# The recurrence's weights loaded from GpSimd's own queue, and a head's output stores tied behind the next head's value products

## The chip, the cores and the metric

The kernel runs on one core of one Trainium2 chip. The metric is the time of one execution on the device in microseconds (us), the median of several runs. In the profile PE is TensorE (matmuls), PEld its weight load, DVE is VectorE, ACT ScalarE, POOL GpSimd and SP SyncE, whose instruction queue (SPq in the profile) issues most of the kernel's transfers.

## The reference

The model is a trunk of two layers on a sequence of 1024 tokens of width 1024 in float32. Layer 0 mixes tokens with forgetting attention (FoX, 16 heads), layer 1 with gated linear attention (GLA, 4 heads, keys of width 128, values of width 256); after each stands a SwiGLU channel mixer. Ahead of every sub-layer the rows are normalised (RMS) and modulated by scale, shift and gate computed from a conditioning vector c by the weights `ada_w`. The change is in layer 1's mixer:

```python
def gated_linear_attention(h, w_in, w_a2, b_a, g_o, w_out):
    proj = h @ w_in
    q, k, v, r, a_lr = jnp.split(proj, ...)          # 512, 512, 1024, 1024, 16 columns
    log_alpha = jax.nn.log_sigmoid(a_lr @ w_a2 + b_a) / GLA_TAU
    b = jnp.cumsum(log_alpha, axis=2)                # within a chunk of 64 tokens, by head
    b_last = b[:, :, -1]
    q_in, k_in = q * jnp.exp(b), k * jnp.exp(-b)
    A = jnp.where(tril, jnp.einsum('bnthk,bnshk->bnhts', q_in, k_in), 0.0)
    o_intra = jnp.einsum('bnhts,bnshv->bnthv', A, v)
    kv = jnp.einsum('bnshk,bnshv->bnhkv', k * jnp.exp(b_last[:, :, None] - b), v)
    # S_n = exp(b_last) * S_{n-1} + kv_n, carried from chunk to chunk
    o = o_intra + jnp.einsum('bnthk,nbhkv->bnthv', q_in, s_prev)
    o = o * lax.rsqrt(jnp.mean(o * o, axis=-1, keepdims=True) + EPS) * g_o
    return (o * jax.nn.silu(r)) @ w_out
```

## The kernel before

All products are made of pairs: a float32 value is split into a high part, rounded to the matmul's type, and a low part, what is left of it. `split` gives the high part to ACT (L163) and the low part to DVE (L164), and `mm3` (L241 to L243) makes a product of three matmuls: high by high, low by high, high by low. On-chip memory is a set of 54 slots of 4 KB a partition; a `Ring` hands the slots of a list out in turn, and a slot's next user waits for its last reader.

Each engine runs its instructions in one order. That order is not written by hand: the program is written once in source order, a scheduler that simulates time then orders each engine's instructions (`schedule_with_timeline_sim=True`), and `tc.issue_after(ins)` ties what stands in its block behind an instruction. DMAs stand in the queue of the engine that issues them, between its other instructions. The core is set up with `dynamic_dma_scratch_size=1024`, bytes reserved for the descriptors of transfers that GpSimd issues.

**Weights.** `load_w` (L194 to L210) loads one weight, 512 KB in either shape: 8 blocks of 128 rows by 128 columns, or 4 blocks of 128 rows by 256 columns. One DMA on SP's queue (L198) puts it into a raw buffer of a ring `wr` of three; ACT copies the high parts (L206), and four subtractions of 128x256 make the low parts (L209), all four or three of them on POOL, in the second case the fourth on DVE. `Weights.next` keeps three weights loaded ahead. The names tell which weight it is: `w__s` are those of keys, queries and gates r, `wv` those of values, `wo` the output weights (`_h` high, `_l` low). The ring, so named, has its readers on ACT, POOL and DVE.

**The stage.** Layer 1 begins at about 1300 us with the norm of the rows: half of the columns at a time, `rms_cols` sums squares on PE (`sp`, L531), DVE and POOL make the inverse root of it (`rs`, L534 and L535), and PE spreads this over partitions (`rb`, L543). Then the modulated rows `h1` are made, `h1h` by ACT (L563) and `h1l`, for the odd blocks, by POOL (L564). The second half of the tokens gets its norm while the products of the first half run. `gv_body` makes the values of a quarter of the tokens (`gv` on PE, split into `gvt`), `a_body` and `gate_z` the decay gates, and `r_proj` the output gate `gr` (Silu into the ring `gs` of two slots).

**The heads.** For each of the four heads `head_front` makes keys (`gk`) and queries (`gqp`). DVE multiplies a projection by the decay into one of two buffers `gy` (L1703 for the queries); from there ACT rounds the high parts (`kih`, `gq00h` and so on) and POOL subtracts the low part of the keys, `kil` (L1688); DVE makes the low part of the queries. So a buffer `gy` is free for the next projection when POOL has made `kil`. `head_back` makes scores (`at`), values under scores (`go`), the state (`kv`, by the transposed keys `kdh`, `kdl`) and the normalised outputs `gs`: the inverse root `gss` is POOL's (L1804), DVE scales, PE transposes (`ogt`, L1764), DVE multiplies it into `gs` (L1767). `head_end` finishes the last of these outputs and, for heads 0 to 2, stores two 128x1024 tiles of them on SP's queue (L1718). They are loaded again when the output product is made; those of head 3 stay on chip.

**Beside it.** Between the heads' instructions runs `ada1`, the modulation of what follows: SP loads a 128x512 tile of `ada_w` in four pieces (L361), ACT multiplies it by the condition (L379), POOL adds it to a sum (L381). Its tiles are a short ring, so SP waits for POOL there. The rows of `x` that the mixer's result is added to are put aside on SP's queue (`x_d`, L1550).

Of the kernel before, what the change touches and what calls it, by code (L numbers as in the profile page):

```python
# [16 lines left out]
P = 128  # L17
# [36 lines left out]
def trunk(ctx, tc, x, c, ada_w, ada_b, norm1_g, norm2_g, ffn_w_in, ffn_w_out,  # L54
          fox_w_in, fox_b_f, fox_w_out, gla_w_in, gla_w_a2, gla_b_a, gla_g_o,
          gla_w_out, final_g, out, dbg=None, stop=None):
    nc = tc.nc
    dbg = dbg or {}
# [53 lines left out]
    def run(g):  # L112
        for _ in g:
            pass
# [4 lines left out]
    def weave(a, ta, b, tb, lags=None):  # L119


        ca = cb = 0.0
        a_on = b_on = True
        bb = nc.cur_bb.bb.instructions
        hist = {e: [] for e in lags or ()}
        while a_on or b_on:
            n = len(bb)
            if a_on and (not b_on or ca * tb <= cb * ta):
                r = next(a, None)
                a_on = r is not None  # L130
                ca += r or 0.0
                for e, h in hist.items():
                    new = [i for i in bb[n:] if i.engine == ENG[e]]
                    h.append(new[-1] if new else h[-1] if h else None)
            else:
                r = next(b, None)
                b_on = r is not None
                cb += r or 0.0
                for e, h in hist.items():
                    if len(h) > lags[e] and h[-1 - lags[e]] is not None:  # L140
                        for i in bb[n:]:
                            if i.engine == ENG[e]:
                                tc.add_manual_dep(i, h[-1 - lags[e]].name, mybir.DependencyInfo(
                                    mybir.DependencyClass.NoSync, mybir.DependencyReason.DATA), reason="order")
# [17 lines left out]
    def split(hi, lo, src):  # L162
        nc.scalar.copy(hi, src)  # L163
        nc.vector.tensor_sub(lo, src, hi.bitcast(F32))  # L164
# [24 lines left out]
    def leave_ffn():  # L189
        if opr_:  # L190
            ws.q = deque(opr_["sg"] + list(opr_["r"].q))
            opr_.clear()

    def load_w(src, name, ws=ws, lo_p=3):  # L194

        kk, m = src.shape[0] // P, src.shape[1]
        raw = wr([P, kk, m], F32, name)
        nc.sync.dma_start(raw, src.rearrange("(k p) m -> p k m", p=P))  # L198
        leave_ffn()
        w = Pair(ws([P, kk, m], FR, name + "h"), ws([P, kk, m], FR, name + "l"))  # L200
        flat = lambda t: t.rearrange("p k m -> p (k m)")
        hi, lo, rw = flat(w.hi), flat(w.lo), flat(raw)
        n = kk * m
        for i in range(2):
            cs = slice(i * n // 2, (i + 1) * n // 2)
            nc.scalar.copy(hi[:, cs], rw[:, cs])  # L206
        for i in range(4):
            cs = slice(i * n // 4, (i + 1) * n // 4)
            (nc.gpsimd if i < lo_p else nc.vector).tensor_sub(lo[:, cs], rw[:, cs], hi[:, cs].bitcast(F32))  # L209
        return w  # L210
# [15 lines left out]
    class Weights:  # L226
# [7 lines left out]
        def next(self):  # L234
            while self.loads and len(self.got) < self.depth:
                f, *a = self.loads.popleft()
                self.got.append(f(*a))
            return self.got.popleft()
# [13 lines left out]
    def proj_tok(ps, w2, hs, t):  # L252

        ts_ = psl(t)
        for k in range(8):
            w = w2[k // 4]
            mm3(ps, hs[k].hi[:, ts_], hs[k].lo[:, ts_], w.hi[:, k % 4, :], w.lo[:, k % 4, :], k == 0, k == 7)
            yield 0.33
# [53 lines left out]
    W = fox_w_in[0]  # L312
    wf = load_w16(W[:, 3 * D:3 * D + 16], "fw", wst)
    wq0 = load_w(W[:, 0:P], "wq0", wst)
    wk0 = load_w(W[:, D:D + P], "wk0", wst)
    load_ada0(1)
    load_ada0(2)
# [27 lines left out]
    def last_of(e, n=0):  # L345
        return [i for i in nc.cur_bb.bb.instructions[-400:] if i.engine == ENG[e]][-1 - n]
# [83 lines left out]
    def ada1_queue(js, acc, raws_, ahead=1):  # L430
        r = Cycle(raws_)
        for j in js:
            ada1.q.append(ada_pair(1, j, lambda *_: acc, r, 1, ahead))
# [210 lines left out]
    def w_loads(wmat, lo, w=P):  # L644
        return [(load_w, wmat[:, lo:lo + w], f"w{lo}_")]
# [920 lines left out]
    ada_v = Views(take(2), 2, [HALF], "ad").v  # L1566
    ada1_queue((2, 4), ada_v[0], ada_v[1:4], 2)
    ADA_A, ADA_B, ADA_LAG = 2.5, 1.0, 6
    rm = cst.tile([P, HALF], BF16, name="rm")
    nc.vector.memset(rm, 1.0)  # L1570
    nc.vector.memset(rm.rearrange("p (n c) -> p n c", c=P)[:, :, 0:1], 0.0)
# [29 lines left out]
    def gv_body(h, wv, tp):  # L1601
        ps = pj([P, 2, 256], F32, f"gv{h}{tp}")
        for i in range(2):
            run(proj_tok(ps[:, i, :], wv, h1, 2 * tp + i))
        ada1(5.1)
        v = vr([P, 2, 2, 256], FR, f"gvt{h}{tp}")
        split(v[:, 0], v[:, 1], ps)
        return v
# [65 lines left out]
    def head_front(h, b16, t2, ei, nmid):  # L1674

        ahead = gate_ahead(h + 1) if h < 3 else iter(())
        wk = feed.next()
        kin = Pair(kir([P, S], FR, f"kih{h}"), kir([P, S], FR, f"kil{h}"))
        for hf in range(2):
            cs = hsl(hf)  # L1680
            ps = pj([P, HALF], F32, f"gk{h}{hf}")
            run(proj(ps, wk, h1, hf))
            ada1(5.1)
            y = yv()
            nc.vector.tensor_mul(y, ps, ei[:, cs])
            nc.vector.tensor_mul(t2[:, cs], ps, t2[:, cs])
            nc.scalar.copy(kin.hi[:, cs], y)
            nc.gpsimd.tensor_sub(kin.lo[:, cs], y, kin.hi[:, cs].bitcast(F32))  # L1688
            for n in range(4 * hf, 4 * hf + 4):
                nc.scalar.activation(ei[:, psl(n)], b16[:, psl(n)], AF.Exp, scale=1.0 / 16, bias=nmid[:, n:n + 1])  # L1690
            nc.scalar.activation(b16[:, cs], b16[:, cs], AF.Exp, scale=1.0 / 16)
            if h:
                next(ahead, None)
        wq = feed.next()
        qt = [Pair(qr([P, S], FR, f"gq{h}{i}h"), qr([P, S], FR, f"gq{h}{i}l")) for i in range(2)]
        for hf in range(2):
            cs = hsl(hf)
            ps = pj([P, HALF], F32, f"gqp{h}{hf}")
            run(proj(ps, wq, h1, hf))
            ada1(5.1)  # L1700
            for t, f in zip(qt, (ei, b16)):
                y = yv()
                nc.vector.scalar_tensor_tensor(y, ps, QS, f[:, cs], op0=ALU.mult, op1=ALU.mult)  # L1703
                split(t.hi[:, cs], t.lo[:, cs], y)
            if not h:
                next(ahead, None)
        return kin, qt
# [4 lines left out]
    def head_end(h, gs):  # L1712

        run(last_og.popleft())
        for dv in range(2):
            gtile[2 * h + dv] = gs[dv]
            if h < 3 or "og" in dbg:
                nc.sync.dma_start(og_d[2 * h + dv], gs[dv])  # L1718

    def head_back(h, kin, qt, t2, dec, vt, gs, need):  # L1720
# [89 lines left out]
    def r_proj(h, gs, done):  # L1810
        wr_ = [None, None]
        for hf, dv in ((0, 0), (0, 1), (1, 0), (1, 1)) if h else ((0, 0), (1, 0), (0, 1), (1, 1)):
            if wr_[dv] is None:
                wr_[dv] = feed.next()
            ps = pj([P, HALF], F32, f"gr{h}{dv}{hf}")
            yield from proj(ps, wr_[dv], h1, hf)
            ada1(5.1)
            nc.scalar.activation(gs[dv][:, hsl(hf)], ps, AF.Silu)
            done.add((dv, hf))
            yield 0.01  # L1820
# [6 lines left out]
    with tc.issue_after(rb_ins[-1]):  # L1827
# [3 lines left out]
        gs = [gsr([P, S], F32, f"gs0{i}") for i in range(2)]  # L1831
# [14 lines left out]
    for h in range(4):  # L1846
        dec, nmid = dec
        kin, qt = head_front(h, b16, t2, ei, nmid)
        if h:
            gs = [gsr([P, S], F32, f"gs{h}{i}") for i in range(2)]  # L1850
            done = set()
            rg = r_proj(h, gs, done)

        def need(dv, g, rg=rg, done=done):
            while (dv, g) not in done:
                next(rg, None)
        weave(head_back(h, kin, qt, t2, dec, vt, gs, need), 13.0, rg, 20.8)
        if h < 3:
            with tc.issue_after(sq_ins[0]):
                b16, t2, ei, dec = gate_exps(h + 1, gnext.pop())  # L1860
            wv = [feed.next(), feed.next()]
            vt = [gv_body(h + 1, wv, 0)]
            head_end(h, gs)
            vt += [gv_body(h + 1, wv, tp) for tp in range(1, 4)]


    ada1.flush()
# [12 lines left out]
    for _ in range(8):  # L1880
        next(first)
    head_end(3, gs)
    for k in (6, 7):
        split(oh[k].hi, oh[k].lo, gtile[k])
# [67 lines left out]
```

## Time and profile before

| | |
|---|---|
| time, 3 runs | 2420.53, 2420.7 and 2425.13 us, median 2420.7 |
| profiled execution | 2425.68 us, its span 2423.9 us |
| mean granted PE clock | 0.993 |
| busy PE, PEld, DVE | 2374.1, 2018.3, 1666.9 us |
| busy ACT, POOL | 1190.8, 1201.3 us |

A row of the groups reads: line, engine, operation, output <- input by the program's names without buffer numbers, tile and type, count. A row of the timeline has the start and the length in us ahead of that, and at the end, in brackets, how long the engine stood idle before it and which instruction released it. A row of the waits has engine, tile and line that waited, then the releaser, then us in total, times and the longest. SPq is SP's queue, whose DMA issues are listed with their count, size and median us from issue to landing.

### The profile page before, as it was taken

To read this page: it belongs to the slowest core of one execution; us is meant where nothing else is said; L and a number is where in the kernel's file an instruction comes from. 1 tells how busy PE (TensorE), PEld (TensorE's weight loads), DVE (VectorE), ACT (ScalarE), POOL (GpSimd) and SP (SyncE) were. 2 spreads that over 40 slices of the span, in tenths; PEclk is the share of its full clock that TensorE was granted. 3 is DMA by queue.
4 is the path that set the end of the run, shared out by engine and by line. 5 is a ranking of instruction groups with operands and counts; after the bars stand their busy time and mean duration, and the time that the engine had idled before them with its cause. 6 is when DMAs were issued, how large, how long until landed. Compare 5 with 4: busy or idle time off the path is not lost.

```text
span 2423.9 us, 36045 instructions
## 1 busy us (share of the span) xinstructions
PE 2374.1 (98%) x12338; PEld 2018.3 (83%) x12338; DVE 1666.9 (69%) x2789; ACT 1190.8 (49%) x2286; POOL 1201.3 (50%) x1071
## 2 busy tenths in 40 slices
PE   7999999999999999999999999999999999999998
PEld 6888888878888888888888788898888888888878
DVE  6577677676687877875797545435587767666687
ACT  4666555675444444445324765653343334345325
POOL 3344344332347878843263555662335656653362
PEclk9999999999999999999999999999999999999999
DMA  9233333133435555457665343444325444347664
GB/s 271 80 108 111 105 106 105 62 96 114 131 103 180 187 165 170 162 193 258 230 194 164 92 120 103 131 121 157 110 88 176 157 135 153 135 171 256 232 202 147
DMA packets 329503, 362.40 MB, mean 150 GB/s; under 512 B 24476, under 2 KB 252984, under 8 KB 329320
## 3 DMA queue, kind: packets, MB, share of 16 engines
q1 hardware_dynamic: 329128, 360.09, 46.0%
q8 instruction: 97, 1.59, 0.3%
q14 instruction: 86, 0.70, 0.1%
q10 hardware_dynamic: 192, 0.02, 0.0%
HBM read 269.78 MB, written 90.24 MB: 149 GB/s over the span
## 4 chain that ended last, share of the span: by engine, by line
PE 80%; DVE 6%; DMA 4%; ACT 3%; POOL 3%; issue 2%; SPq 1%; DVEq 0%; POOLq 0%; ACTq 0%
PE p_b L241 15%; PE p_b L243 15%; PE p_b L242 15%; PE o_b L971 2%; PE t_b L957 2%; PE qk_b L241 2%; PE qk_b L243 2%; PE qk_b L242 2%; PE s_b L926 1%; PE s_b L927 1%; PE gr_b L241 1%; PE gr_b L243 1%; PE gr_b L242 1%; PE vps_b L242 1%; PE vps_b L241 1%
## 5 line engine op out<-in xcount | busy, mean ns | idle before, releaser
L164 DVE TENSOR_TENSOR o_s<-xv_s,o_s 128x512 fp32r<-128x512 f32 (+1 forms) x376 | 338.5, 903 | 81.1 <-ACT o_s L163 79.9
L163 ACT CAST o_s<-xv_s 128x512 fp32r<-128x512 f32 (+1 forms) x376 | 217.8, 586 | 318.6 <-PE p_b L243 245.2
L242 PE MATMUL p_b<-B,o_s 128*128 128x512 f32 x608 | 237.9, 391 | 0.0
L243 PE MATMUL p_b<-B,o_s 128*128 128x512 f32 x608 | 237.2, 391 | 0.0
L241 PE MATMUL p_b<-B,o_s 128*128 128x512 f32 x608 | 236.8, 392 | 0.0
L937 POOL TENSOR_SCALAR lp_s<-lp_s,st 128x128 f32<-128x128 f32 (+7 forms) x128 | 97.5, 766 | 267.8 <-DVE st L936 250.1
L704 POOL TENSOR_TENSOR ex_s<-xv_s,xv_s 128x512 f32<-128x512 f32 (+1 forms) x64 | 87.1, 1361 | 266.6 <-DMA xv_s<-in_ffn_w_in_dram 101.4
L241 PE MATMUL p_b<-T,o_s 128*128 128x512 f32 x480 | 186.7, 389 | 0.0
L242 PE MATMUL p_b<-T,o_s 128*128 128x512 f32 x480 | 186.7, 389 | 0.0
L243 PE MATMUL p_b<-T,o_s 128*128 128x512 f32 x480 | 180.7, 389 | 0.0
L243 PEld LDWEIGHTS p_b<-B,o_s 128*128 128x128 f32 x608 | 114.8, 189 | 24.1
L242 PEld LDWEIGHTS p_b<-B,o_s 128*128 128x128 f32 x608 | 115.0, 189 | 23.7
L241 PEld LDWEIGHTS p_b<-B,o_s 128*128 128x128 f32 x608 | 115.0, 189 | 23.7
L935 ACT ACTIVATE lp_s<-lp_s,st 128x128 f32<-128x128 f32 (+7 forms) x128 | 99.3, 776 | 65.4 <-DVE st L931 63.2
L381 POOL TENSOR_TENSOR ad_s<-ad_s,ad_s 128x512 f32<-128x512 f32 x62 | 89.0, 1436 | 56.3 <-ACT ad_s L379 40.8
L163 ACT CAST pt_s<-t_b 128x512 fp32r<-128x512 f32 (+1 forms) x160 | 79.6, 547 | 73.8 <-PE t_b L957 73.2
L1309 DVE TENSOR_TENSOR ex_s<-ex_s,p_b 128x512 f32<-128x512 f32 x140 | 94.2, 681 | 28.3 <-PE p_b L243 28.0
L706 POOL TENSOR_TENSOR xv_s<-ex_s,xv_s 128x512 f32<-128x512 f32 (+1 forms) x64 | 85.6, 1338 | 56.0 <-DVE o_s L164 53.7
L164 DVE TENSOR_TENSOR pt_s<-t_b,pt_s 128x512 fp32r<-128x512 f32 (+1 forms) x160 | 96.8, 631 | 13.8 <-ACT pt_s L163 13.5
L243 PEld LDWEIGHTS p_b<-T,o_s 128*128 128x128 f32 x480 | 90.1, 188 | 18.8
L241 PEld LDWEIGHTS p_b<-T,o_s 128*128 128x128 f32 x480 | 90.1, 188 | 18.7
L242 PEld LDWEIGHTS p_b<-T,o_s 128*128 128x128 f32 x480 | 90.1, 188 | 18.7
(1949 smaller groups left out, 7501.3 us busy)
## 6 DMA issues: line engine op xcount, KB each, us to landing
xv_s<-in_ffn_w_in_dram SPq DMA_DIRECT2D x176, 256.0 KB, 3.1
hid_B<-x SPq DMA_DIRECT2D x70, 512.0 KB, 2.7
ad_s<-in_ada_w_dram SPq DMA_DIRECT2D x384, 64.0 KB, 2.0
hid_T<-x SPq DMA_DIRECT2D x36, 512.0 KB, 2.8
xv_s<-in_ffn_w_out_dram SPq DMA_DIRECT2D x96, 192.0 KB, 5.1
ada_s<-in_ada_w_dram SPq DMA_DIRECT2D x128, 128.0 KB, 2.7
xv_s<-in_ffn_w_out_dram SPq DMA_DIRECT2D x40, 256.0 KB, 2.8
T2o<-hid_T SPq DMA_DIRECT2D x18, 512.0 KB, 9.0
```

What stands on the lines that cost most here:

```text
L163: nc.scalar.copy(hi, src)
L164: nc.vector.tensor_sub(lo, src, hi.bitcast(F32))
L241: nc.tensor.matmul(ps, ah, bh, start=start, stop=False)
L242: nc.tensor.matmul(ps, ah, bl, start=False, stop=False)
L243: nc.tensor.matmul(ps, al, bh, start=False, stop=stop)
L381: nc.gpsimd.tensor_add(acc, acc, raw)
L704: nc.gpsimd.tensor_add(s1, a21, a22)
L706: nc.gpsimd.tensor_sub(a11, s1, a11)
L935: nc.scalar.activation(lp, lp, AF.Exp, bias=mcur, scale=-1.0, accum_out=st[:, qi, 2:3])
L937: nc.gpsimd.tensor_scalar(lp, lp, st[:, qi, 3:4], 1.0, op0=ALU.mult, op1=ALU.mult)
L957: nc.tensor.transpose(tp[:, i, :], lps[qi][:, psl(2 * b + jj)], ident)
L1309: nc.vector.tensor_add(d, d if src is None else dest(G, src), ps)
```

## The change

Two things. First, from the point where the recurrence's stage is set up, `load_w` issues a weight's load on GpSimd's queue instead of SP's, in pieces of four row blocks: a weight of eight blocks is two DMAs of 256 KB, one of four blocks a single DMA of 512 KB. This is true of 34 weights: 16 become pairs, 18 singles, 50 DMAs in all. The value weights of head 0 are loaded before that point, and the small weight of the gate has a function of its own; both stay on SP. Second, the stores of a head's outputs leave `head_end`, which stood behind the first quarter of the next head's values, for `head_store`, called behind the fourth quarter and tied to the last TensorE instruction written before it.

```diff
+    pooled = [False]
+
     def load_w(src, name, ws=ws, lo_p=3):
 
         kk, m = src.shape[0] // P, src.shape[1]
         raw = wr([P, kk, m], F32, name)
-        nc.sync.dma_start(raw, src.rearrange("(k p) m -> p k m", p=P))
+        src = src.rearrange("(k p) m -> p k m", p=P)
+        if pooled[0]:
+            for k0 in range(0, kk, 4):
+                nc.gpsimd.dma_start(raw[:, k0:k0 + 4], src[:, k0:k0 + 4])
+        else:
+            nc.sync.dma_start(raw, src)
         leave_ffn()
...
     ADA_A, ADA_B, ADA_LAG = 2.5, 1.0, 6
+    pooled[0] = True
     rm = cst.tile([P, HALF], BF16, name="rm")
...
         run(last_og.popleft())
         for dv in range(2):
             gtile[2 * h + dv] = gs[dv]
-            if h < 3 or "og" in dbg:
+
+    def head_store(h, gs):
+        with tc.issue_after(last_of("P")):
+            for dv in range(2):
                 nc.sync.dma_start(og_d[2 * h + dv], gs[dv])
...
             head_end(h, gs)
             vt += [gv_body(h + 1, wv, tp) for tp in range(1, 4)]
+            head_store(h, gs)
```

The added lines shift the line numbers: L209 before is L216 after, L564 is L571, L1688 is L1696. POOL's order at the entry to layer 1 was, ahead of the inverse root `rs` of the second half (`w__s` are the raw weights of queries, keys and gates, `w_l_s` their low parts, x2 and x4 rows in a run):

```order
L217 MEMSET aw_s_85_12988 128x1024
L564 TENSOR_TENSOR h1l_12678<-te_s_12503,h1h_12677 128x512
L564 TENSOR_TENSOR h1l_12682<-te_s_12504,h1h_12681 128x512
L209 TENSOR_TENSOR w_l_s_87_12995<-w__s_95_12992,w_h_s_86_12994 128x256 x4
L564 TENSOR_TENSOR h1l_12686<-te_s_12505,h1h_12685 128x512
L564 TENSOR_TENSOR h1l_12690<-te_s_12506,h1h_12689 128x512
L535 TENSOR_TENSOR rs_12917<-rs_12917,mhalf 128x4
```

and is now, at the same place:

```order
L224 MEMSET aw_s_85_12988 128x1024
L203 DMA w__s_95_12992<-in_gla_w_in_dram 128x4x128 x2
L571 TENSOR_TENSOR h1l_12678<-te_s_12503,h1h_12677 128x512
L571 TENSOR_TENSOR h1l_12682<-te_s_12504,h1h_12681 128x512
L571 TENSOR_TENSOR h1l_12686<-te_s_12505,h1h_12685 128x512
L216 TENSOR_TENSOR w_l_s_87_12996<-w__s_95_12992,w_h_s_86_12995 128x256 x2
L203 DMA w__s_97_13173<-in_gla_w_in_dram 128x4x128 x2
L571 TENSOR_TENSOR h1l_12690<-te_s_12506,h1h_12689 128x512
L216 TENSOR_TENSOR w_l_s_87_12996<-w__s_95_12992,w_h_s_86_12995 128x256 x2
L203 DMA w__s_96_13003<-in_gla_w_in_dram 128x4x128 x2
L203 DMA w__s_98_13402<-in_gla_w_in_dram 128x4x128 x2
L542 TENSOR_TENSOR rs_12917<-rs_12917,mhalf 128x4
```

Four pairs of loads have come in: one ahead of the first `h1l`, one ahead of the last, and two ahead of `rs`. On PE the sums of squares `sp` of the second half moved with it. In the row where they now begin stood the product of the values that needs the last `h1l`:

```order
L242 MATMUL gv_b_1_13012<-wv_4l_s_84_12878,h1h_12689 128x256
L243 MATMUL gv_b_1_13012<-wv_4h_s_83_12877,h1l_12690 128x256
L241 MATMUL gv_b_1_13012<-wv_0h_s_81_12852,h1h_12675 128x256
L242 MATMUL gv_b_1_13012<-wv_0l_s_82_12853,h1h_12675 128x256
L243 MATMUL gv_b_1_13012<-wv_0h_s_81_12852,h1l_12676 128x256
```

and now it reads:

```order
L249 MATMUL gv_b_1_13014<-wv_4l_s_84_12878,h1h_12689 128x256
L538 MATMUL sp_b_1_12900<-ones,se_s_12502 128x1
L538 MATMUL sp_b_1_12900<-ones,se_s_12500 128x1
L538 MATMUL sp_b_1_12900<-ones,se_s_12501 128x1
L538 MATMUL sp_b_1_12900<-ones,se_s_12499 128x1
```

Before, the sums came 25 rows later, behind the rest of the values' products; the spreading matmuls `rb` (L543) moved up by 18 rows as well. In the heads POOL's order ahead of `kil` was, in head 1 (`ad_s` are the sums of `ada1`):

```order
L209 TENSOR_TENSOR w_l_s_105_14338<-w__s_104_14335,w_h_s_104_14337 128x256 x4
L381 TENSOR_TENSOR ad_s_12964<-ad_s_12964,ad_s_12965 128x512
L1688 TENSOR_TENSOR kil_s_4_14230<-gy_s_12962,kih_s_3_14229 128x512
L381 TENSOR_TENSOR ad_s_12964<-ad_s_12964,ad_s_12965 128x512
L381 TENSOR_TENSOR ad_s_12964<-ad_s_12964 128x512
L381 TENSOR_TENSOR ad_s_12964<-ad_s_12964,ad_s_12965 128x512
L209 TENSOR_TENSOR wv_0l_s_107_14443<-wv_0_s_105_14440,wv_0h_s_106_14442 128x256 x4
L1688 TENSOR_TENSOR kil_s_4_14230<-gy_s_12962,kih_s_3_14229 128x512
```

and is now:

```order
L216 TENSOR_TENSOR w_l_s_105_14346<-w__s_104_14342,w_h_s_104_14345 128x256 x4
L203 DMA wv_4_s_106_14538<-in_gla_w_in_dram 128x4x256
L388 TENSOR_TENSOR ad_s_12964<-ad_s_12964,ad_s_12965 128x512
L203 DMA w__s_107_14818<-in_gla_w_in_dram 128x4x128 x2
L1696 TENSOR_TENSOR kil_s_4_14237<-gy_s_12962,kih_s_3_14236 128x512
L388 TENSOR_TENSOR ad_s_12964<-ad_s_12964,ad_s_12965 128x512
L216 TENSOR_TENSOR wv_0l_s_107_14451<-wv_0_s_105_14448,wv_0h_s_106_14450 128x256 x2
L388 TENSOR_TENSOR ad_s_12964<-ad_s_12964 128x512
L216 TENSOR_TENSOR wv_0l_s_107_14451<-wv_0_s_105_14448,wv_0h_s_106_14450 128x256 x2
L1696 TENSOR_TENSOR kil_s_4_14237<-gy_s_12962,kih_s_3_14236 128x512
```

A single load and a pair have come in ahead of the first `kil`; the second has one sum less ahead of it. SP's queue loses the 34 loads: its rows behind the small gate weight (L222) are now the stores of `x_d` and then the loads of `ada_w`, close together.

## The prediction

> **What bounds the kernel now.** I read the page first, then a table of windows over the stage that is touched, then the waits of each engine in it, and last the timelines at the places where an instruction moves.
>
> ```profile
> span 2423.9 us, 36045 instructions
> ...
> PE 2374.1 (98%) x12338; PEld 2018.3 (83%) x12338; DVE 1666.9 (69%) x2789; ACT 1190.8 (49%) x2286; POOL 1201.3 (50%) x1071
> ```
>
> TensorE is busy 98% of the span, GpSimd (POOL) half of it. The change acts from about 1300 us, where layer 1 begins, to about 1740 us. The windows of that stretch, whose columns are the window, its length, busy time of PE, PEld, DVE, ACT and POOL with counts, the granted clock, the DMA share and GB/s:
>
> ```profile
> 1300.00:1400.00 100.00, 93.64 (x511) 81.26 (x511) 57.40 (x78) 69.88 (x122) 57.76 (x57) 0.95 0.40 119
> 1400.00:1480.00 80.00, 75.67 (x477) 67.50 (x476) 42.87 (x67) 48.37 (x106) 50.69 (x48) 1.00 0.46 134
> 1480.00:1740.00 260.00, 258.81 (x1479) 226.40 (x1478) 119.17 (x197) 127.88 (x269) 119.77 (x127) 1.00 0.38 116
> ```
>
> PE idles 6.4 + 4.3 + 1.2 = 11.9 us in 440; at a clock of 0.95 the first window costs some 5 us more. Whatever the change does on other engines, it can give back no more than about 17 us, and less than that if it makes nothing arrive earlier that PE waits for. What PE waits for is in the waits (waiting engine and line, releaser, us, times, longest), with two rows of other engines below:
>
> ```profile
> PE at_b L241 <- ACT gq00h_s L163: 2.6, 1, 2.6
> PE kv_b L241 <- ACT kdh_s L163: 2.2, 1, 2.2
> PE gr_b L241 <- DVE gvt_s L164: 1.8, 1, 1.8
> PE gv_b L243 <- POOL h1l L564: 1.8, 2, 1.2
> ...
> SPq L1718 <- DVE gs_s L1767: 23.5, 3, 12.9
> ...
> ACT ad_s L379 <- DMA ad_s<-in_ada_w_dram: 40.2, 22, 4.2
> ```
>
> None of PE's waits ends on a weight load or on SP. SP's queue does hold things up (23.5 us ahead of the stores of a head's outputs, at most 12.9 at once), and what feels it is ACT, which waits 40.2 us for modulation weights that stand behind on SP. But one of PE's waits ends on POOL: the products of the values (gv_b) wait for h1l, and two more pass through POOL a step earlier (gq00h and kdh, below). So POOL is the engine that must not be late, and the change gives it work.
>
> **The change part by part.** The 34 loads cost SP one issue each and POOL nothing. Now POOL issues 16 of them as a pair of 256 KB pieces and 18 as one piece of 512 KB, 50 in all. The nearest rows for an issue and a landing:
>
> ```profile
> L198 SPq DMA_DIRECT2D w__s<-in_gla_w_in_dram x16: 368/386/522, 1305.5 to 1581.1; - x16
> ...
> 1326.26 1.02 POOL L535 TENSOR_TENSOR rs<-rs,mhalf 128x4 f32<-128x4 f32 x1 [8.57 <-DVE rs L534]
> ...
> ad_s<-in_ada_w_dram SPq DMA_DIRECT2D x384, 64.0 KB, 2.0
> ...
> xv_s<-in_ffn_w_out_dram SPq DMA_DIRECT2D x40, 256.0 KB, 2.8
> ...
> w__s<-in_gla_w_in_dram SPq DMA_DIRECT2D x16, 512.0 KB, 4.0
> ```
>
> No row shows POOL issue a load. An issue costs between 0.38 us (SP's) and 1.02 us (the smallest operation that POOL does here); I take 1.0, since POOL starts even 128x4 numbers in no less. The kernel reserves 1,024 bytes for descriptors of such loads, and the change cuts a weight into pieces of 512 rows; my choice is that one piece fills that room, so that a piece close behind another holds POOL until the first has landed. That wait is the landing less SP's 0.4: 2.8 - 0.4 = 2.4 us for 256 KB, with 0 (there is room) and 4.0 - 0.4 = 3.6 (the 512 KB row) as ends; the 64 KB row would give 1.6. A pair then costs POOL 1.0 + 2.4 + 1.0 = 4.4 us (ends 2.0 and 5.6). The Trainium skill, DMA: Bandwidth & Descriptors, section "Anatomy of one DMA — SWDGE (gpsimd) path", fits such a load with 2.0 us and a term by bytes, 2.6 us for 256 KB by my estimate; with it the wait would be 1.6 us and the sum below some 14 us instead of 19. The trace has that kind of load nowhere, so I keep the 256 KB row.
>
> *Entry.* POOL now has a pair ahead of h1l, one ahead of the last h1l, and two ahead of the inverse root rs.
>
> ```profile
> 1307.58 3.02 POOL L564 TENSOR_TENSOR h1l<-te_s,h1h 128x512 fp32r<-128x512 f32 x2
> 1310.55 4.17 POOL L209 TENSOR_TENSOR w_l_s<-w__s,w_h_s 128x256 fp32r<-128x256 f32 x4
> 1314.69 2.99 POOL L564 TENSOR_TENSOR h1l<-te_s,h1h 128x512 fp32r<-128x512 f32 x2
> ...
> 1317.74 0.39 PE L243 MATMUL gv_b<-wv_4h_s,h1l 128*128 128x256 f32 x1 [0.52 <-POOL h1l L564]
> ...
> 1319.82 0.67 DVE L586 TENSOR_TENSOR se_s<-se_s 128x512 f32<-128x512 f32 x1
> ...
> 1322.31 3.67 PE L531 MATMUL sp_b<-ones,se_s 128*128 128x1 f32 x30
> ...
> 1330.89 1.05 PE L543 MATMUL rb_b<-ident,rs 128*128 128x128 f32 x8
> ```
>
> From 1307.6: pair to 1312.0, two h1l to 1315.0, one to 1316.5, two subtractions (half of 4.17) to 1318.6, pair to 1323.0, last h1l to 1324.5. PE's sum of squares (sp_b) now stands ahead of the product that needs this h1l: it starts when se is there, 1320.5, and ends at 1324.2. The product starts at 1324.5, and the stretch from it to where sp_b began, 1322.3 - 1317.7 = 4.6 us, ends at 1329.1 against 1326.0: 3.1 us late. POOL goes on: subtractions to 1326.6, pair to 1331.0, wait 2.4, pair to 1337.8, rs to 1338.8. PE reaches rb_b, which moved up by 18 rows of 4.6/24 = 0.19 us, at 1330.9 + 3.1 - 3.4 = 1330.6 and waits 8.2 us. Together 11.3; of the 1.8 us in which gr_b waits for gvt I let 1.3 fall into this. Entry: **+10.0**.
>
> *Heads.* Ahead of a head's first kil (low part of its keys) POOL gets one or two single pieces and a pair, in heads 0 to 2; head 3 has only a single. kil frees the buffer gy in which DVE puts the queries (0.69 us) that ACT rounds (0.60 us) for at_b.
>
> ```profile
> 1360.31 10.24 POOL L209 TENSOR_TENSOR w_l_s<-w__s,w_h_s 128x256 fp32r<-128x256 f32 x12
> 1372.52 1.29 POOL L381 TENSOR_TENSOR ad_s<-ad_s 128x512 f32<-128x512 f32 x1 [1.97 <-issue]
> ...
> 1375.15 1.30 POOL L1688 TENSOR_TENSOR kil_s<-gy_s,kih_s 128x512 fp32r<-128x512 f32 x1
> ...
> 1381.31 0.60 ACT L163 CAST gq00h_s<-gy_s 128x512 fp32r<-128x512 f32 x1
> ...
> 1452.04 1.30 POOL L1688 TENSOR_TENSOR kil_s<-gy_s,kih_s 128x512 fp32r<-128x512 f32 x1
> ...
> 1459.58 5.20 POOL L209 TENSOR_TENSOR wv_0l_s<-wv_s,wv_0h_s 128x256 fp32r<-128x256 f32 x4 [1.53 <-ACT wv_0h_s L206]
> 1464.75 1.29 POOL L1688 TENSOR_TENSOR kil_s<-gy_s,kih_s 128x512 fp32r<-128x512 f32 x1
> ...
> 1466.07 0.69 DVE L1703 SCALAR_TENSOR_TENSOR gy_s<-gqp_b,b_s 128x512 f32<-128x512 f32 x1 [1.94 <-POOL kil_s L1688]
> ...
> DVE gy_s L1703 <- POOL kil_s L1688: 3.9, 2, 1.9
> ...
> 1531.29 5.60 POOL L209 TENSOR_TENSOR w_l_s<-w__s,w_h_s 128x256 fp32r<-128x256 f32 x8
> 1536.86 1.29 POOL L1688 TENSOR_TENSOR kil_s<-gy_s,kih_s 128x512 fp32r<-128x512 f32 x1
> ...
> 1548.65 1.29 POOL L1688 TENSOR_TENSOR kil_s<-gy_s,kih_s 128x512 fp32r<-128x512 f32 x1
> ```
>
> Head 0: subtractions end at 1370.6; single 1.0; short wait 1.0 and single 1.0; one modulation add 1.3; wait 2.4 - 1.3 = 1.1; pair 4.4; kil 1.3 ends at 1381.7 (before 1376.5). Most of this uses up the old 1.97 us of idleness and 3 us of slack; gy and its rounding end at 1382.9 against 1381.9: **+1.0**. Head 1: single 1.0 and, after an add, wait 1.1 and pair 4.4: the first kil ends 6.5 us later, at 1459.8; then add, two subtractions (half of 5.20), add, two subtractions, kil: 1.3 + 2.6 + 1.3 + 2.6 + 1.3 to 1468.9 against 1466.0. DVE waits for this very kil today (3.9 us in two heads), so there is no slack: **+2.9**. Head 2: 1.0 + 2.4 + 4.4 = 7.8 ahead of the first kil, which ends at 1546.0; two adds and four subtractions of 2.8 (half of 5.60) to 5.2, kil: 1552.7 to 1555.1 against 1549.9, in the middle **+4.0**.
>
> *Tail.* The pieces of the output weights that stand ahead of the last inverse root gss:
>
> ```profile
> 1673.03 2.50 POOL L209 TENSOR_TENSOR wo_512l_s<-wo_s,wo_512h_s 128x256 fp32r<-128x256 f32 x3 [6.40 <-ACT wo_512h_s L206]
> ...
> 1678.14 0.69 POOL L1804 TENSOR_TENSOR gss<-gss,mhalf 128x2 f32<-128x2 f32 x1
> 1682.94 0.27 PE L1764 MATMUL ogt_b<-ident,on_t 128*128 128x128 f32 x1
> ```
>
> Four pieces and three waits, 4.0 + 7.2 = 11.2 us, against 6.4 of idleness: gss some 4.8 late, of which the 4.1 us between its end and ogt_b take most: **+1.0**.
>
> *Stores and SP.* SP loses 34 issues (34 x 0.38 = 13 us) and the stores' wait of 23.5 us. It ends no wait of PE, so I book 0 for it; ACT's 40.2 us are the cover, and the second rival is what it is worth if they matter. The six stores only move behind the products of the next values.
>
> Sum: 10.0 + 1.0 + 2.9 + 4.0 + 1.0 = 18.9 us. On the profiled execution, 2425.7 us (1.8 more than its span), that is 2444.6. That execution lies 5.0 us over the median of 2420.7, so on the median's basis **2439.6**. A measurement can tell about 0.2%, 4.8 us, from no change.
>
> **The rivals.** *1. Room enough: no piece waits.* A pair costs 2.0. Entry: the last h1l ends at 1319.7, PE's stretch starts at 1324.2 behind sp_b: +2.8, and rs in time. Head 1: kil's subtractions still start at 1459.6, with one more add behind: +1.3, head 2 the same. Sum 5.4: 2426. For it: POOL idles half the time, and ends most idle stretches on ACT. Against: pieces, and 1,024 bytes.
>
> *2. Faster: SP's queue was the hidden bound.* The modulation loads no longer stand behind weights and stores, ACT's 40.2 us of waiting shrink, and with them PE's waits on ACT's gq00h and kdh (2.6 + 2.2) and some of the 5 us of clock and 1.8 of gvt: about -8, 2413. It decides if a piece costs POOL below some 0.7 us with no wait and kil stays in time. For it: PE's waits do pass through ACT. Against: POOL is in the same chain, a step earlier, and loses what ACT wins.
>
> *3. Worse: a piece holds POOL as long as 512 KB take, 3.6 us, so a pair 5.6.* Worked as above: entry +16.0, heads +4.3, +5.3 and +6.4, tail +5: 37 us, 2458. For it: four subtractions take 5.20 us at 1459.6 and 10.24/3 = 3.4 us at 1360.3, so POOL's work stretches beside others'. The Trainium skill, SBUF — State Buffer, section "SBUF: two separate sides", warns that a load from GpSimd's queue can't get its descriptors written while VectorE holds the port that they share; by that rule the delays here would be larger still, and no row shows such a load beside VectorE.
>
> **How the numbers follow.** Forecast (pieces wait for a landing) 0.46; room enough 0.22; faster 0.20; worse 0.12. The forecast's own range is 2435 to 2449 (a wait of 1.6 to 3.0 us between pieces, the sum taken in proportion between the cases worked above). Room enough, at 2426, lies on the bound of no change (2420.7 + 4.8 = 2425.5): 0.12 of it go to same, 0.10 to slower. So faster 0.20, same 0.12, slower 0.68. The range leaves out half of the faster case (0.10, below 2413) and the far part of the worse one (0.08, above 2456).
>
> **What would show it.** Right: in 1300 to 1345 us PE waits 6 us or more ahead of rb_b for POOL's rs, with POOL idle or issuing ahead of it; second pieces issued 3 us or more behind first ones; kil of heads 1 and 2 ends 3 us later with DVE's wait on it grown; the stores' 23.5 us on SP gone and the time no better for it. Wrong: pairs issued within 2 us; rb_b unwaited for; PE's waits on gq00h and kdh gone, which would be the faster case.

## The result and the profile after

The changed kernel takes 2461.8 us, the median of five runs, against 2423.1 us for the kernel before, beside it. The ratio is 1.0159, with a 95% interval of 1.0143 to 1.0175. It is slower, as forecast, but by 38.7 us where the sum said 18.9, and 5.8 us above the upper end of the range. The profiled execution took 2460.71 us, 35.0 more than the one before, which lay 2.5 us over its median.

The page of the changed kernel, with the new queue (packets, MB, share of 16 engines):

```profile
span 2458.9 us, 36102 instructions
...
PE 2383.6 (97%) x12338; PEld 2025.6 (82%) x12338; DVE 1676.4 (68%) x2789; ACT 1191.7 (48%) x2286; POOL 1230.8 (50%) x1121
...
q0 software_dynamic: 5152, 17.83, 2.4%
```

POOL is busy 29.5 us more: the issues make 38.6 (50 of 0.77), and its other operations took some 9 less. No engine has much more to do. PE stands still instead. The windows of the stage, in the columns used for before:

```profile
1300.00:1400.00 100.00, 82.49 (x431) 73.06 (x430) 50.90 (x66) 58.45 (x106) 52.90 (x58) 0.87 0.31 93
1400.00:1480.00 80.00, 74.27 (x455) 65.86 (x454) 33.84 (x58) 47.03 (x97) 46.44 (x51) 0.98 0.38 111
1480.00:1775.00 295.00, 282.09 (x1572) 244.24 (x1571) 142.04 (x217) 140.43 (x291) 158.22 (x173) 0.99 0.38 116
```

PE idles 17.5 + 5.7 + 12.9 = 36.1 us in 475, against 11.9 in 440 before, and in the first window its granted clock is 0.87 where it was 0.95. For about as many matmuls (2,458 against 2,467) it is busy 438.9 us instead of 428.1, so the waits come with a second cost, slower matmuls. What it waits for, and what POOL waits for:

```profile
PE go_b L248 <- ACT ahl_s L163: 6.1, 3, 4.3
PE sp_b L538 <- DVE se_s L593: 5.0, 1, 5.0
PE at_b L248 <- ACT gq00h_s L163: 3.7, 1, 3.7
PE ogt_b L1775 <- DVE on_t L1817: 3.6, 2, 2.3
PE gv_b L248 <- DVE gvt_s L164: 3.5, 1, 3.5
PE kv_b L248 <- ACT kdh_s L163: 3.4, 2, 2.4
PE rb_b L550 <- POOL rs L542: 3.3, 1, 3.3
...
POOL w__s L203 <- issue: 61.8, 21, 3.8
...
SPq L1729 <- DVE gs_s L1778: 24.4, 3, 11.4
```

The row of POOL is what the forecast was made of: POOL stood 61.8 us in front of loads of w__s for nothing that the profile shows, 21 times, 2.9 us each on average. The first pair, and the last one with rs behind it, in POOL's timeline:

```profile
1306.41 0.97 POOL L203 DMA_DIRECT2D w__s<-in_gla_w_in_dram  x1
1310.24 0.77 POOL L203 DMA_DIRECT2D w__s<-in_gla_w_in_dram  x1 [2.87 <-issue]
...
1336.59 0.75 POOL L203 DMA_DIRECT2D w__s<-in_gla_w_in_dram  x1 [2.87 <-issue]
1337.36 1.03 POOL L542 TENSOR_TENSOR rs<-rs,mhalf 128x4 f32<-128x4 f32 x1
```

A later pair costs POOL 0.77 + 2.8 + 0.75 = 4.3 us (forecast 4.4), and rs ends at 1338.4 (forecast 1338.8). Such pieces land in a median of 3.3 us from issue. The trace also says what POOL waits for: of the 49 loads that follow another one, 27 start 0.30 to 0.31 us after the landing of the load before, whatever its size, and none starts before that landing. Added up, POOL's waits ahead of these 27 are 75 us; the profile puts some of them down to other engines.

To see where the rest went, I took the start of the same matmul in both traces. The column of growth is what each step adds to PE's lag:

| matmul | before | after | lag | growth | forecast |
|---|---|---|---|---|---|
| first product of the values, head 0 | 1312.1 | 1311.3 | -0.8 | | |
| third quarter of these values | 1345.0 | 1354.1 | 9.1 | 9.9 | 10.0 |
| first product of head 0's keys | 1361.0 | 1376.3 | 15.3 | 6.2 | 0 |
| second block of head 0's scores | 1388.8 | 1405.7 | 16.9 | 1.6 | 1.0 |
| first product of head 1's keys | 1442.8 | 1465.4 | 22.6 | 5.7 | 0 |
| first product of head 2's keys | 1528.8 | 1557.7 | 28.9 | 6.3 | 2.9 |
| first product of head 3's keys | 1611.6 | 1645.9 | 34.3 | 5.4 | 4.0 |
| first output product | 1667.8 | 1702.1 | 34.3 | 0 | 0 |
| near the end | 2412.8 | 2447.1 | 34.4 | 0.1 | 1.0 |

The first step came out at 9.9 us where 10.0 was forecast, and rs, which sets its end, at the time that was worked out. But PE spent that time otherwise. The sum had it wait 8.2 us ahead of rb_b:

```profile
1322.37 6.56 PE L538 MATMUL sp_b<-ones,se_s 128*128 128x1 f32 x30 [4.98 <-DVE se_s L593]
...
1338.44 1.65 PE L550 MATMUL rb_b<-ident,rs 128*128 128x128 f32 x8 [3.27 <-POOL rs L542]
```

It waited 3.3 us there. The sums of squares had started 1.9 us later than forecast, and they took 6.56 us instead of 3.67, with a granted clock of 0.67 from 1320 to 1340 us, where it was 0.87 before. The two figures agree more closely than their parts do.

Two steps have no term in the sum. In the first, ACT rounds the values (gvt) behind the decays' exponentials, and PE, which needs the buffer back, stands:

```profile
1365.13 1.32 ACT L386 ACTIVATE ad_s<-ad_s,cblk 128x512 f32<-128x512 f32 x2
1366.35 0.56 ACT L163 CAST gvt_s<-gv_b 128x512 fp32r<-128x512 f32 x1
...
1367.69 0.58 PE L248 MATMUL gv_b<-wv_0h_s,h1h 128*128 128x256 f32 x1 [3.54 <-DVE gvt_s L164]
```

In the second, a pair and three sums of `ada1` stand ahead of an inverse root gss whose input DVE had ready at 1429.1:

```profile
1427.15 0.77 POOL L203 DMA_DIRECT2D w__s<-in_gla_w_in_dram  x1 [1.54 <-issue]
1430.68 0.75 POOL L203 DMA_DIRECT2D w__s<-in_gla_w_in_dram  x1 [2.76 <-issue]
...
1434.06 0.73 POOL L1815 TENSOR_TENSOR gss<-gss,mhalf 128x2 f32<-128x2 f32 x1
...
1434.82 0.88 DVE L1817 TENSOR_SCALAR on_t<-go_b,gss 128x256 f32<-128x256 f32 x2 [5.68 <-POOL gss L1815]
```

Of this wait 2.3 us reach PE at the transposes (ogt_b, at 1435.5). And in head 1 the second kil was late about as forecast (it ends at 1491.1, 25.1 us later than before, of which PE's lag by then was 22.6), but one difference on DVE then took 5.73 us instead of some 0.7:

```profile
1491.14 0.69 DVE L1711 SCALAR_TENSOR_TENSOR gy_s<-gqp_b,b_s 128x512 f32<-128x512 f32 x1 [5.82 <-POOL kil_s L1696]
...
1498.57 5.73 DVE L164 TENSOR_TENSOR gq10l_s<-gy_s,gq10h_s 128x512 fp32r<-128x512 f32 x1
...
1504.96 0.62 ACT L163 CAST ahl_s<-atz_s 128x512 fp32r<-128x512 f32 x1 [2.38 <-DVE atz_s L1749]
```

Behind the late kil PE waits 2.0 us, for the low part of the queries. Its longest wait in this head, 4.3 us ahead of go_b, is for this ahl, whose input DVE masked (atz) right behind the long difference.

### The profile page after: what moved, and what is told of

Same layout as the page of the kernel before. It is cut to its first block, busy times and chain, and to the rows that moved or that the text cites. A ratio compares the mean times of both kernels' runs of the same rounds, so it can differ in the third digit from the quotient of the medians.

```text
span 2458.9 us, 36102 instructions
## 1 busy us (share of the span) xinstructions
PE 2383.6 (97%) x12338; PEld 2025.6 (82%) x12338; DVE 1676.4 (68%) x2789; ACT 1191.7 (48%) x2286; POOL 1230.8 (50%) x1121
## 4 chain that ended last, share of the span: by engine, by line
PE 82%; DVE 4%; issue 3%; DMA 3%; POOL 3%; ACT 2%; SPq 1%; POOLq 0%; DVEq 0%; ACTq 0%
PE p_b L250 15%; PE p_b L248 15%; PE p_b L249 15%; PE o_b L978 2%; PE t_b L964 2%; PE qk_b L248 2%; PE qk_b L250 2%; PE qk_b L249 2%; PE s_b L933 1%; PE s_b L934 1%; PE vps_b L249 1%; PE vps_b L248 1%; PE vps_b L250 1%; PE gv_b L250 1%; PE gv_b L248 1%
## 5 line engine op out<-in xcount | busy, mean ns | idle before, releaser
L1316 DVE TENSOR_TENSOR ex_s<-ex_s,p_b 128x512 f32<-128x512 f32 x140 | 93.9, 680 | 29.0 <-PE p_b L250 28.9
```

The lines of the kernel that those rows point to most:

```text
L1316: nc.vector.tensor_add(d, d if src is None else dest(G, src), ps)
```

## The experiments

Theory: a piece fills the room for descriptors, the next one close behind holds POOL until it has landed, and what waits for POOL is late. Rivals: the queue takes one load at a time whatever the room; the new order of the instructions costs by itself; the loads' absence from SP, or the stores, matter.

### Twice the room

```diff
-dynamic_dma_scratch_size=1024
+dynamic_dma_scratch_size=2048
-    tri = cst.tile([P, P], I32, name="tri")
+    tri = cst.tile([P, P], mybir.dt.uint8, name="tri")
-    rm = cst.tile([P, HALF], BF16, name="rm")
+    rm = cst.tile([P, HALF], mybir.dt.uint8, name="rm")
...
```

> The changed kernel with 2,048 bytes for descriptors instead of 1,024 (two small masks are held as bytes to make the space); every engine's instructions stand in the same order as in the changed kernel. If a piece waits on POOL because the one before it fills the room (my reading of the changed kernel: 2.8 us ahead of each second piece, 62 us in all), a pair's second piece now goes out behind the first, a pair costs 1.6 us instead of 4.4, and most of the 38.7 us go: 5 to 15 us over before are left, what the new order of the instructions costs. If POOL always waits for the load before it (a queue with one load under way, whatever the room), nothing changes: +36 to +41. If the order itself, made by the scheduler, is the cause, at least 20 us stay although the waits are gone.

Measured: 2440.2 us, ratio 1.0060 (1.0041 to 1.0079), that is 16 us over the 2424.1 of the kernel before beside it. POOL's idle time ahead of loads, by what ended it (us, times), fell from 65.2 to 1.6 in the row that the first theory speaks of (the changed kernel first):

```profile
  issue: 65.2, 23
...
  issue: 1.6, 2
```

POOL's timeline shows how many pieces now fit:

```profile
1320.87 2.25 POOL L203 DMA_DIRECT2D w__s<-in_gla_w_in_dram  x3 [2.27 <-DVE w2t L164]
1324.53 0.76 POOL L203 DMA_DIRECT2D w__s<-in_gla_w_in_dram  x1 [1.41 <-issue]
```

Three go out one behind the other and the fourth waits; it starts 0.31 us after the landing of the first of them. The order of the instructions is the same on every engine as in the changed kernel, so the room alone is worth some 22 us of the 38.7. The queue is not one that takes a single load: 27 loads are issued here before the load ahead of them has landed. The 16 that are left are a little above the expected 5 to 15. They can come from the order, from the issues themselves and from long operations of DVE, which this kernel still has (see the last section); they were not told apart here.

### The late rounding of the values

```diff
     gate_sum(0, bt, (0,))
-    gate_exps(0, bt, (0,), to0)
     vt.append(gv_body(0, wv, 2))
+    with tc.issue_after(last_of("A")):
+        gate_exps(0, bt, (0,), to0)
```

on top of the kernel with twice the room:

> The kernel with 2,048 bytes for descriptors, with one thing more: the products of the third quarter of head 0's values are written ahead of the first half's decays, which are tied behind the rounding of these values (gvt), so that ACT rounds them ahead of the decays' exponentials as it did before the change. With the room alone, ACT rounds gvt some 5 us later, behind the exponentials and two modulation tiles; PE waits 3.5 us for it and its lag grows by 5.3 us between 1351 and 1361 us. If the order of ACT is the cause, that growth falls below 1.5 us and the kernel is 3 to 6 us faster than with the room alone: +8 to +12 over before. If PE would have been slow there anyway (the clock after the waits at the entry), 2 us or less are gained.

Measured: 2432.7 us, ratio 1.0047 (1.0032 to 1.0061): 9 over before. That is 7 us below the room alone by the differences to the kernel before and 3 by the ratios, whose intervals overlap; in the traces the last matmul starts 6.4 us earlier. PE's wait for gvt there, which is this row with the room alone,

```profile
PE gv_b L248 <- DVE gvt_s L164: 3.5, 1, 3.5
```

is not in the trace any more, and the lag between the third quarter of the values and the keys grows by 0.2 us instead of 5.3. So the late rounding costs something by itself, and the loads brought it about only through the scheduler. The edit does not move that rounding alone: the products of the third quarter also stand ahead of the decays' on PE, and 49 matmuls and 6 operations of POOL have changed their places. The same edit with 1,024 bytes:

> The changed kernel (1,024 bytes for descriptors) with the third quarter's values written ahead of the first half's decays, so that ACT rounds gvt ahead of the exponentials as before the change. With more room this took 7.5 us off. If the late rounding of gvt is a cause of its own, it takes off about as much here: 2452 to 2457, and PE's wait for gvt (3.5 us) goes. If POOL's waits cover it here (what PE gains it loses again at the next kil), less than 2 us go.

Measured: 2458.8 us, ratio 1.0152 (1.0129 to 1.0175). That is 2 us less than the changed kernel by the ratios and 4 by the differences to the kernel before, with an interval of 5.6 us to either side, so the time does not decide. In the trace the growth at the values is gone (0.2 us), but PE's wait at the scores is longer:

```profile
PE at_b L248 <- ACT gq00h_s L163: 5.9, 1, 5.9
```

It was 3.7. PE comes earlier to queries that POOL's kil still holds back. It is 6.8 us ahead of the changed kernel at head 0's keys and 3.9 at the first output product. While POOL waits, a part of what the rounding gives is lost again; the steps do not simply add up.

### Entry and heads apart

A count of the loads decides: in the first kernel weights 5 to 34 go to POOL, in the second weights 1 to 4.

```diff
-        if pooled[0]:
+        if pooled[0]:
+            n_pool[0] += 1
+        if pooled[0] and n_pool[0] > 4:     # the other kernel: n_pool[0] <= 4
```

> The change without its entry: the first four weights (the pairs ahead of h1l and rs) stay on SP's queue, the 30 others and the stores are as changed. The lag of PE in the traces grows by 9.9 us up to the norm of the second half, 6.2 in the values behind it and 1.6 at the first scores. If the entry's pairs cause all of the first two, about 16 us go: +20 to +25 over before. If the pieces of the heads alone decide (entry's delay is recovered later, since POOL's work just runs later), less than 5 us go: +34 to +38.

> Only the first four weights (the four pairs at the entry) on GpSimd's queue, the other 30 on SP's; the stores as changed. PE's lag grew by 9.9 us at the norm and 6.2 in the values behind it in the changed kernel; the kernel without these four was at +27. If the steps add up, this one is at +38.7 - 27 = about 12 us, 10 to 18 over before. If the heads' lags only take what the entry's left (POOL catches up), it is nearer to +25.

Measured: without the entry's pairs 2450.8 us, ratio 1.0109 (1.0088 to 1.0129), 27 over before; with these alone 2439.6 us, ratio 1.0062 (1.0038 to 1.0085), 16 over. Together 43 against 38.7, so the two add up but for some 4 us. The entry alone is where it was expected; without it 12 us go instead of about 16. The waits of that kernel suggest why:

```profile
PE at_b L250 <- ACT gq00h_s L163: 11.2, 1, 11.2
```

PE comes to the scores of head 0 earlier and waits there three times as long (3.7 in the changed kernel).

### Smaller parts on POOL

In one kernel the first half of a pair is issued on POOL and the second on SP; in the other POOL issues only the first block of 128 rows of each weight.

```diff
-                nc.gpsimd.dma_start(raw[:, k0:k0 + 4], src[:, k0:k0 + 4])
+                (nc.sync if k0 else nc.gpsimd).dma_start(raw[:, k0:k0 + 4], src[:, k0:k0 + 4])
```

> The change with the second piece of each pair on SP's queue and the first on POOL's; a single piece stays on POOL. POOL's issues fall from 50 to 34, and no piece stands right behind another of the same weight; 1,024 bytes for descriptors as in the changed kernel. If what costs is the wait of a second piece for the first, nearly all of the 62 us of POOL's waits go and the time is that of the kernel with more room or a little less: +8 to +16 over before. If every load on POOL's queue costs by itself (its issue, or taking it off SP), it falls in proportion to the issues, by 16 of 50: +24 to +28.

```diff
-            for k0 in range(0, kk, 4):
-                nc.gpsimd.dma_start(raw[:, k0:k0 + 4], src[:, k0:k0 + 4])
+            nc.gpsimd.dma_start(raw[:, 0:1], src[:, 0:1])
+            nc.sync.dma_start(raw[:, 1:], src[:, 1:])
```

> The change with POOL issuing only the first block of 128 rows of each of the 34 weights (64 or 128 KB) and SP the other blocks; POOL's order is near that of the kernel with halves, the issues at the same places. If the room for descriptors is what makes POOL wait, a block of 128 rows leaves room for three more and POOL's waits ahead of its loads are 0 to 3 us in all, the time +4 to +12 over before. If POOL waits for each load to land whatever its rows, 1 us or more stays ahead of each load that follows another closely and the time is as with halves, +15 or more. On VectorE's long operations: if a POOL load's descriptors take them, their number falls with the rows (none above 2.5 us); if it is POOL's order that lies against VectorE's, they are as in the kernel with halves (6.5 us at the entry).

Measured: halves 2442.8 us, ratio 1.0081 (1.0057 to 1.0105), 19 over before, which lies between the two ranges that were named; the first block alone 2430.4 us, ratio 1.0037 (1.0023 to 1.0052), 9 over. Halves first (POOL's waits), then the block (line L202, durations in ns of each issue):

```profile
POOL w__s L203 <- issue: 14.5, 4, 3.9
```

```profile
L202 POOL DMA_DIRECT2D w__s<-in_gla_w_in_dram x16: 534/562/762, 1308.8 to 1588.2; - x16
```

With halves 14.5 us of waiting stay in this row, where pieces of different weights come close behind one another; with 128 rows none is put down to issue, and 9 loads go out before the load ahead has landed. That agrees with the room and speaks against a wait for each landing. An issue of 128 rows costs 0.56 us, one of 512 rows 0.77.

### The loads, the stores and the queue by themselves

The loads alone (the stores as before), the stores alone (no load on POOL, the first edit shown) and the loads on ACT's queue (the second):

```diff
-    pooled[0] = True
```

```diff
-                nc.gpsimd.dma_start(raw[:, k0:k0 + 4], src[:, k0:k0 + 4])
+                nc.scalar.dma_start(raw[:, k0:k0 + 4], src[:, k0:k0 + 4])
```

> Only the loads on GpSimd's queue; the stores stand in head_end as before. My prediction booked nothing for the stores: +36 to +41 as with both. A rival: the stores behind the values' products free SP for the modulation loads, and without it the loads-only kernel is slower still, by 3 us or more; or the stores are what pushes the heads' order about, and it is faster by 3 us or more.

> Only the stores moved behind the next values' products; all loads on SP's queue as before. My prediction: within 3 us of before, since PE waits neither for SP nor for the stores. Rival: SP's 23.5 us ahead of the stores were the cause of ACT's waits for modulation weights, and this alone is 3 to 8 us faster than before.

> Once more only the stores moved, with more rounds, since it read 0.15% below before with an interval that holds no change. Booked at 0: within 3 us of before. Rival: the stores' place is worth something, 2 to 6 us faster than before with an interval wholly below 1.

> The change with the same pieces on ACT's queue instead of GpSimd's; the stores as changed. POOL then issues nothing, as before, and SP is rid of the loads just as in the change. If taking the loads off SP is worth something (my second rival, 8 us at most), it shows here: -2 to -8 against before. If nothing waits for SP (booked at 0) and ACT, half idle, issues 50 pieces at about the 0.4 us that SP takes, the time is within 4 us of before, or a little slower where ACT stands behind a full buffer: -2 to +6.

Measured: the loads alone 2464.1 us, ratio 1.0164 (1.0141 to 1.0187), the same as both. The stores alone 2421.7 us, ratio 0.9985 (0.9967 to 1.0004), and again 2422.4 us, ratio 0.9996 (0.9982 to 1.0009): nothing. The loads on ACT 2423.3 us, ratio 1.0001 (0.9989 to 1.0014): nothing either, though ACT waits less for its modulation weights, 25.6 us instead of 40.2:

```profile
ACT ad_s L386 <- DMA ad_s<-in_ada_w_dram: 25.6, 16, 4.9
...
L203 ACTq DMA_DIRECT2D w__s<-in_gla_w_in_dram x32: 374/387/1412, 1303.2 to 1575.5; - x32
```

So with SP rid of the loads nothing is gained, as booked, or no more than ACT's 50 issues of 0.39 us take back, and the harm is POOL's. None of these kernels beats the kernel before clearly.

### A load with nothing in it

```diff
+        nc.sync.dma_start(raw, src)
+        if pooled[0]:
+            n = len(probes)
+            probes.append(probe[0:1, 2 * n:2 * n + 2])
+            nc.gpsimd.dma_start(probes[-1], src[0:1, 0, 0:2])
```

> All loads on SP's queue as before and the stores as changed, but with each of the 34 weights POOL issues one load of 8 bytes, into a place of its own that nothing reads. In every kernel whose POOL issues loads, single VectorE operations near them took 2 to 6.5 us (a 128x512 difference 5.73 us, 1.85 us at most in the kernel before). If a POOL load's issue does that by itself, operations over 2 us are here too and the time is 5 us or more over before. If it takes the 512 rows of descriptors, or POOL's work piled up behind its waits, there are none, POOL's issue of a load costs below 0.76 us, and the time is within 5 us of before.

Measured: 2434.0 us, ratio 1.0046 (1.0028 to 1.0063). This one missed its aim:

```profile
L206 POOL DMA_DIRECT2D probe<-in_gla_w_in_dram x22: 518/518/742, 1.8 to 15.4; - x22
L206 POOL DMA_DIRECT2D probe<-in_gla_w_out_dram x12: 518/521/579, 16.9 to 38.2; - x12
```

Nothing ties these loads, so the scheduler put all of them into the first 40 us, and the 10 us are lost there: PE is some 11 us late by 95 us and 13 at the end. No operation of DVE in the stage took over 1.9 us, but no POOL load stood beside them either, so it says nothing on that question. It does give the price of an issue without a payload, 0.52 us.

## Why the prediction was right and wrong

**Right: the mechanism and its price.** A pair was put at 4.4 us and measured 4.3, by two errors that offset: the issue is 0.77 and not 1.0, the wait 2.8 and not 2.4. The 1.0 was taken from rs as POOL's smallest operation, while the row of gss, 0.69 us, stood in the same prediction. The other wait that was weighed, 1.6, was not worked out like the sum's own: a landing of 2.6 us less 0.4 is 2.2. That the wait comes from the room for descriptors was a choice between two readings; twice the room took it away. The end of the entry, rs, was worked out within 0.4 us. Its 9.9 us for 10.0 owe something to luck, since PE waited 3.3 us at rb_b and not 8.2 and lost the rest in later and slower sums. Head 0's kil was put at 1.0 against 1.6, the second kil of head 1 at 2.9 late against 2.5; head 3 and the tail were about 0. The stores and SP were booked at 0, which kernels of their own show. Two signs of being right did not come: PE's wait of 6 us or more ahead of rb_b, and the end of SP's wait of 23.5 us ahead of the stores, which is 24.4 with the change and costs nothing either.

**Wrong: the sum looked only at POOL's rows ahead of h1l, rs and kil.** Three things are missing from it. First, 6.2 us behind the entry: I took the order of PE and POOL as changed and ACT's as it was, and even let 1.3 us of PE's wait for gvt vanish. In the new order ACT has gvt behind the nine operations of the exponentials and two tiles of the modulation. With more room, putting it back gained 3 to 7 us; at 1,024 bytes a part of that is lost again at the next wait. Second, 5.7 us in head 0's outputs: a pair stands ahead of gss there, and I worked out such a wait only for the tail. That gss held DVE 5.7 us, and PE 2.3 of them, is in the trace; that this makes the whole lag is not shown. Third, head 1's lag of 6.3 and not 2.9: kil was late as forecast, and PE's 4.3 us ahead of go_b go with DVE's difference of 5.73 us. Head 2 was 5.4 for 4.0. There the pair stands behind a single piece of 512 KB, and the sum took the wait of a 256 KB piece, 2.4; it was 3.7, and the pieces ahead of the first kil took 8.9 us instead of 7.8. Whether that is all of it is open. With 18.9 + 6.2 + 5.7 + 3.4 + 1.4 the sum is 35.6, and PE's lag grew by 35.2. This names the steps that were missed, but it is no second proof, since the added terms are read from that same lag.

**The rivals.** Room enough did not hold, and its price was too low as well: the kernel that has the room is 16 over before, not 5.4, in part since the rounding's place costs without any wait of POOL. The faster case fell with the loads on ACT's queue, where SP is just as free of them and nothing is gained. The worse case came nearest in time (2458), but for another reason: behind a piece of 256 KB POOL waits 2.8 us, not 3.6. The range ended too low because its upper end was made of dearer pieces, and not of places that the sum had left out.

## What to carry to other kernels

Before loads go to an engine that also computes, count its rows ahead of every value that another engine waits for, the small ones (an inverse root of 128x2) as well as the large; half idle on average says nothing about those places. Look for the room its descriptors have: a piece that fills it turns the next issue into a wait for a landing, here nearly four times as dear as the issue (2.9 against 0.77 us). Where a scheduler sets the order, read the difference on all engines, since an edit to one queue moved a rounding on another engine, and putting that back gained 3 to 7 us once the wait was gone.

## What the runs showed of the hardware

GpSimd's issue of a load took 0.52 us for 8 bytes, 0.56 for 128 rows and 0.77 for 512; on SP and ACT it is 0.39. With 1,024 bytes one piece of 512 rows was under way at a time, with 2,048 at most three. The next issue came 0.3 us after the landing that it waited for.

Not expected: single operations of VectorE stretched where POOL issued loads. In the kernel before none in the stage took over 1.85 us; after the change there were two of about 6 us, the one shown in head 1 and this, and one of 3.8 in head 2:

```profile
1310.67 6.04 DVE L565 SCALAR_TENSOR_TENSOR h1l<-te_s,modc,h1h 128x512 fp32r<-128x512 f32 x1
1311.03 3.76 POOL L571 TENSOR_TENSOR h1l<-te_s,h1h 128x512 fp32r<-128x512 f32 x3
1314.74 1.41 POOL L216 TENSOR_TENSOR w_l_s<-w__s,w_h_s 128x256 fp32r<-128x256 f32 x2
1316.11 0.77 POOL L203 DMA_DIRECT2D w__s<-in_gla_w_in_dram  x1
```

It started within POOL's issue and ended within the next one, while POOL's own operations between ran at their usual 1.3 and 0.7 us. Every kernel with POOL loads in the stage has some (with twice the room one of 5.9 in head 1 and one of 5.3 at the entry; with 128 rows 3.8 at the entry and one of 2.6 behind the heads); the stores alone and the loads on ACT have none above 1.9. The Trainium skill, SBUF — State Buffer, section "SBUF: two separate sides", describes the opposite, VectorE keeping descriptors from being written; here the issues kept to 0.75 to 0.97 us and it was VectorE's operations that took longer. The page also says that whichever of VectorE and GpSimd starts first holds a port that they share for its whole instruction; why VectorE would be held up over several of POOL's instructions is open. In the kernel before, twelve subtractions of POOL lay back to back for 10.24 us from 1360.3, and no operation of VectorE beside them took over 1.65 us; that speaks for the issue, but whether the issue does it, or POOL's work behind it, was not told apart.

The granted clock of TensorE was lower where it waited more: 0.87 in the first 100 us of the stage where before it was 0.95. An idle microsecond there came with more than its own cost.
